# The low half of the w1 weights: a negated copy on ScalarE and a DMA that adds, in place of a subtraction on VectorE

## The chip, the cores and the metric

The kernel runs on one core of one Trainium2 chip. The metric is device time of one launch in microseconds (us); the median of three runs before the change is 1082.82 us (1081.4 to 1083.72). The core's engines are called PE (TensorE, the matrix unit; PEld is its weight load), DVE (VectorE), ACT (ScalarE), POOL (GpSimd) and SP (SyncE, which here does nothing but issue DMAs).

## What is computed

Two residual layers on an input of 512 tokens by 1024 features, all in float32. Layer 0 mixes tokens by a state-space scan and an attention with forget gates, layer 1 by a causal pooling and a gated unit. After each mixer stands a dense MLP with a squared ReLU, and that is where the change lies. Cut to what matters:

```python
for l in range(2):
    h = rms_norm(x, mix_pre_g[l])
    y = even_mixer(h, ...) if l % 2 == 0 else odd_mixer(h, ...)
    x = x + rms_norm(y, mix_post_g[l])
    h = rms_norm(x, mlp_pre_g[l])
    y = jnp.square(jax.nn.relu(h @ w1[l])) @ w2[l]     # w1: 1024 x 4096, w2: 4096 x 1024
    x = x + rms_norm(y, mlp_post_g[l])
```

## The kernel before, in words

**Two halves of every number.** PE multiplies in a float32 format of reduced precision (`fp32r`). To keep the precision, each operand is split in two: `hi`, the value rounded to fp32r, and `lo = value - hi`. `split` (line 611) does it: ACT copies the source to `hi`, which rounds, and DVE subtracts `hi` from the source into `lo`. `mm3` (line 620) then makes one product from three matmuls, hi by hi, hi by lo, lo by hi, accumulated in one PSUM bank.

**Weights.** A weight piece is a tile of 128 partitions by 1024 columns (512 KB). `class W` (line 634) takes three SBUF slots (`hi`, `lo`, `raw`), lets SP load the piece into `raw`, splits it, and frees `raw`. A w1 piece is the 1024 x 128 column block of w1 for 128 hidden features; in DRAM its rows are 128 floats, so it comes in 1024 runs of 512 bytes. There are 32 pieces for each of the two MLPs. w2 pieces are only loaded here (`Raw`); they are combined and split later.

**The MLP.** `mlp` (line 893) goes through four quarters of the hidden features. In each, eight times: take one w1 piece, compute its 128 x 512 hidden block (`block_T`, 24 matmuls), square the ReLU (`finish`), and between those blocks the second matrix product is done by seven block products in place of eight (`Seven`: `begin`, `corner`, and at the quarter's end `end` or, for the last quarter, `tail`). In the first quarter the first four pieces of MLP 0, three of MLP 1 (`FIRST`), are taken together, half of the tokens at a time, so that work can begin while the boundary before is still finishing.

**Order of the work.** Nothing runs when it is recorded. `Program.record` collects all operations, and `Program.issue` (line 284) simulates the five engines with fixed prices (`cost`, lines 242 to 282, and the latencies in `LAT`) and picks for each engine, one after the other, the ready operation of the best priority. The result is a fixed instruction order for every engine; on the chip each engine runs its list in that order and waits where an operand is not ready. A priority is made of the place in the program, the length of the chain that hangs on the operation, and hand-tuned boosts. In the planner's prices a 512 KB load on SP occupies the DMA for 1.6 us (`v.shape[0] * free(v) * 4 / 330`) and lands 2.0 us after that (lines 380 to 383, with 60 ns for the issue).

**Slots.** The tiles share 47 slots of 1024 columns and 4 of 512 (`Slots`, `Room`). A tile gets its slot when its first operation is picked, and how far a tile may run ahead of the oldest tile that has no slot yet is bounded by `LOOKS` (line 37): for loads, 7 tiles in MLP 0 (phase 1) and 13 in MLP 1 (phase 3). `take` and `getw` record up to `DEPTH` = 5 pieces ahead of their use.

**POOL's work.** In the MLPs POOL does almost nothing. At the layer boundaries it computes `1/sqrt` of the mean square (`rstd_of`, line 762), two small operations per norm.

Of the kernel before, what the change touches and what calls it, by code (L numbers as in the profile page):

```python
# [38 lines left out]
POOLF = 1  # L39
NWARM = 16  # L40
RANK = 0.55
DUE = 0.0
ORDER = "f z c q0 a0 u o q1 t s0 a1 s1 q2 a2 s2 q3 a3 s3".split()
ACTI = [3]
PBOOST = 4
# [121 lines left out]
class Program:  # L167
# [73 lines left out]
    @staticmethod  # L241
    def cost(eng, name, outs, ins, args, kw):
        def free(v):
            n = 1
            for x in v.shape[1:]:
                n *= x
            return n

        n = max([free(v) for v in outs[:1] + ins if v.shape[0] > 1 or len(ins) < 2] or [1])
        psum = any(v.t.bank for v in ins)  # L250
        if eng == "PE":
            out = outs[0]
            cols = free(out)
            if name == "transpose":
                return 109
            if ins[0].dtype == F32 and ins[0].t.dt != BF16:
                half = out.shape[0] <= 64 and ins[0].shape[0] <= 64
                return max(80, cols * 1.08) if half else cols * 1.7
            if ins[0].t.dt == BF16 or out.shape[0] <= 64:
                return max(53, cols / 2.4 + 3)  # L260
            return max(107, cols / 2.4 + 13.4)
        if eng == "ACT":
            ptr = sum(isinstance(kw.get(k), View) for k in ("bias", "scale", "accum_out"))
            return 0.833 * n + (51 if psum else 93) + 90 * ptr
        if eng == "DVE":
            if name == "reciprocal":
                return 6.3 * n + 60
            fast = name in ("tensor_copy", "tensor_scalar") and not psum
            ptr = 0
            if name in ("tensor_scalar", "scalar_tensor_tensor"):  # L270
                ptr = sum(isinstance(a, View) for a in args[2:4]) - (name == "scalar_tensor_tensor")
            return (0.52 if fast else 1.04) * n + 67 + 64 * ptr
        if eng == "POOL":
            if kw.get("op") == ALU.pow:
                return 464
            if name == "memset":
                return 0.83 * n + 36
            return 1.85 * n + 150 + 85 * (name == "tensor_scalar" and isinstance(args[2], View))
        if outs:
            v = outs[0]  # L280
            return v.shape[0] * free(v) * 4 / 330.0
        return 1600

    def issue(self):
# [7 lines left out]
                p.succs.append(o)  # L292
        for o in reversed(ops):
            o.rank = o.ns + max((s_.rank + self.LAT[o.eng][s_.eng] for s_ in o.succs), default=0.0)

        at = 0.0
        for o in ops:
            o.due = at
            if o.eng == "PE":
                at += o.ns  # L300
        for o in reversed(ops):
            own = o.due if o.eng == "PE" or not o.succs else math.inf
            o.due = min([own] + [s_.due - self.LAT[o.eng][s_.eng] - o.ns for s_ in o.succs])
        for o in ops:
            if o.eng != "SP":
                o.prio = (1 - DUE) * (o.prio * (1 - RANK) * UNIT - RANK * o.rank) + DUE * o.due - 1e3 * o.boost
                if o.banks and o.eng != "PE":
                    o.prio -= 1e3 * PBOOST
            for t in o.tiles:
                if t.pos is None:  # L310
                    t.pos = len(t.room.users)
                    t.room.users.append(t)
                    t.state, t.left = 0, len(t.ops)
                    t.used = {}
                    if t.bank:
                        t.needs = set(id(p) for u in t.ops if u.eng == "PE" for p in u.preds.values() if p.num < o.num)
# [32 lines left out]
        while len(order) < total:  # L349
            moved = True  # L350
            while moved:
                moved = False
                for e in self.engines:
                    if clock[e] > now:
                        continue
                    pick, best = None, None
                    for o in avail[e]:
                        if o.ready <= now and o.wake <= now and not (e == "SP" and head and o is not head[0]):
                            wake = 0.0
                            for t in o.banks:  # L360
                                for e2, end in t.used.items():
                                    if e2 != e:
                                        wake = max(wake, end + self.LAT[e2][e])
                            if wake > now:
                                o.wake = wake
                                heapq.heappush(events, (wake, len(order) + 0.75, None))
                                continue
                            key = o.prio
                            if e == "PE" and o.banks and o.banks[0].state == 1:
                                key -= STICKY * 1e3  # L370
                            if (best is None or key < best) and may(o):
                                pick, best = o, key
                    if pick is None:
                        continue
                    o = pick
                    avail[e].remove(o)
                    if o in head:
                        head.remove(o)
                    o.start = now
                    if e == "SP":  # L380
                        clock[e] = now + 60
                        dma = max(dma, now) + o.ns
                        o.end = dma + 2000
                    elif e == "PE":
                        while window < int(now / WINDOW):
                            slow, work = (2.0 if work < HAMT else 1.0), 0.0
                            window += 1
                        ns = o.ns
                        if half is not None and (half[1] <= o.half[0] or o.half[1] <= half[0]):
                            ns, half = min(ns, 67), None  # L390
                        else:
                            half = o.half
                        work += o.work
                        clock[e] = o.end = now + ns * slow
                    else:
                        clock[e] = o.end = now + o.ns
                    for t in o.tiles:
                        if t.state == 0:
                            t.room.take(t, e)
                        t.left -= 1  # L400
                        if not t.left:
                            t.room.give(t, self.LAT)
                    for t in o.banks:
                        t.used[e] = max(t.used.get(e, 0.0), o.end)
                    order.append(o)
                    moved = True
                    heapq.heappush(events, (o.end, len(order), o))
                    heapq.heappush(events, (clock[e], len(order) + 0.5, None))
                    for s_ in o.succs:
                        s_.ready = max(s_.ready, o.end + self.LAT[e][s_.eng])  # L410
                        s_.left -= 1
                        if not s_.left:
                            avail[s_.eng].append(s_)
                            heapq.heappush(events, (s_.ready, len(order) + 0.25, None))
            if len(order) == total:
                break
            if not events:
                raise RuntimeError("the schedule is stuck at " + str(len(order)))
            now = max(now, events[0][0])
            while events and events[0][0] <= now:  # L420
                o = heapq.heappop(events)[2]
                if o is not None:
                    done.add(id(o))
# [109 lines left out]
def tile_trunk(ctx: ExitStack, tc: tile.TileContext, x, mix_pre_g, mix_post_g, mlp_pre_g, mlp_post_g,  # L533
# [98 lines left out]


    class W:
        def __init__(self, src, shape):
            n = shape[0] * shape[1]
            self.shape = shape
# [4 lines left out]
            raw = arena.alloc(n)  # L642
            kept = boosted(f"W{prog.phase}")
            SP.dma_start(raw.f().rearrange("p (a b) -> p a b", a=shape[0]), src)
            split(raw.f(), self.b[0].r(), self.b[1].r())
            prog.boost = kept
            raw.free()

# [5 lines left out]
        def free(self):  # L654
            for b in self.b:
                b.free()

    class Raw:

# [26 lines left out]
    def plan_mlp(l):  # L686
        p = []
        for q in range(4):
            first = FIRST[l] if q == 0 else 0
            p += [rows(w1[l], 0, 8, 128 * j, 128) for j in range(first)]  # L690
            for j in range(8):
                if j >= first:
                    p.append(rows(w1[l], 0, 8, 128 * (8 * q + j), 128))
                for m_ in (int(c[1]) for c in AFTER[j].split() if c[0] == "b"):
                    p += [rows(w2[l], 128 * (8 * q + 2 * m_ + k), 1, 0, 1024) + (Raw,) for k in range(2)]
        return p
# [1259 lines left out]
```

## Time and profile before

| | |
|---|---|
| median of three runs | 1082.82 us (1081.4 to 1083.72) |
| the profiled execution | 1084.49 us |
| its span, first to last instruction | 1082.7 us |
| mean granted TensorE clock | 0.989 |
| instructions | 13916 |
| bytes read from HBM | 101.55 MB |

The page of the profile gives busy time by engine, the chain of work that ended last, groups of equal instructions with their mean duration, and DMA issues with the time to landing. Almost every instruction stands under line 429, the line of the planner that emits them, so the rows are told apart by engine, operation and shape: a row `b<-b,b 128x1024 fp32r<-128x1024 f32` on DVE is the subtraction of a split, `b<-b 128x1024 fp32r<-128x1024 f32` on ACT is its rounding copy. Since every engine's list is fixed, the n-th instruction of an engine in the trace is the n-th of its list, and so a single w1 piece can be followed through the trace from its load to the matmul that reads it. The two MLPs lie at about 277 to 577 us and 749 to 1071 us of the span.

### The profile page before, as it was taken

Reading aid. Unit: us, or ns where it says so; the run is one execution under the profiler, and the core shown is the slowest. Engines: PE = TensorE matmul, PEld = TensorE weight load, DVE = VectorE, ACT = ScalarE, POOL = GpSimd, SP = SyncE. Lnnn points to the kernel's source line nnn. Section 1 sums busy time; section 2 is a strip of 40 time slices with the busy share of each in tenths; the row PEclk is TensorE's granted clock in tenths of the full one; section 3 lists DMA queues with packets and bytes.
Section 4 is the critical chain, followed back from the end, with each engine's and each line's share of the span. In section 5 each row is a group of like instructions: output and inputs, shape, how many; then the busy total and the mean of one; then the engine's idle time right before and its main releaser. Section 6 shows DMA issues by size and latency. Waiting matters only on the chain.

```text
span 1082.7 us, 13916 instructions
## 1 busy us (share of the span) xinstructions
PE 1044.6 (96%) x5133; PEld 848.6 (78%) x5133; DVE 783.8 (72%) x1293; ACT 566.8 (52%) x1033; POOL 112.7 (10%) x238
## 2 busy tenths in 40 slices
PE   7979999999999999999999799999999999999997
PEld 4757877688988888888888578878888888888885
DVE  5955879858676497677677998757684686775786
ACT  5525877646474373454463654435663653553551
POOL 2892400003000000000000210011000000000001
PEclk9989999999999999999999899999999999999999
DMA  8122002353303233332423533307022424224302
GB/s 255 41 60 59 20 21 78 110 183 114 99 25 102 90 117 98 103 111 78 137 97 108 156 98 114 120 1 214 21 81 81 150 78 137 97 66 139 107 20 78
DMA packets 110386, 104.54 MB, mean 97 GB/s; under 512 B 9736, under 2 KB 92844, under 8 KB 110318
## 3 DMA queue, kind: packets, MB, share of 16 engines
q1 hardware_dynamic: 110318, 103.66, 31.0%
q8 instruction: 40, 0.66, 0.2%
q14 instruction: 28, 0.23, 0.1%
HBM read 101.55 MB, written 2.10 MB: 96 GB/s over the span
## 4 chain that ended last, share of the span: by engine, by line
PE 79%; DVE 8%; POOL 6%; ACT 3%; issue 2%; SPq 1%; DMA 1%; DVEq 0%; POOLq 0%; ACTq 0%
PE bank L429 79%; DVE b L429 7%; POOL b L429 4%; POOL small L429 2%; ACT junk L429 2%; ACT b L429 1%; SPq L429 1%; DMA b<-in_x_dram 1%; DVE small L429 0%; DVEq L1952 0%; POOLq L1952 0%; ACTq L429 0%; ACTq L1952 0%; DVEq L429 0%; POOLq L429 0%
## 5 line engine op out<-in xcount | busy, mean ns | idle before, releaser
L429 PE MATMUL bank<-b,b 128*128 128x512 f32 (+5 forms) x4684 | 1003.6, 377 | 16.1 <-DVE b L429 6.7
L429 PEld LDWEIGHTS bank<-b,b 128*128 128x128 f32 (+2 forms) x4684 | 812.0, 188 | 190.4 <-ACT b L429 10.2
L429 DVE TENSOR_TENSOR b<-b,b 128x512 fp32r<-128x512 f32 (+5 forms) x622 | 475.7, 800 | 131.1 <-ACT b L429 61.5
L429 ACT ACTIVATE b<-b 128x1024 fp32r<-128x1024 f32 (+6 forms) x578 | 376.0, 693 | 289.1 <-PE bank L429 144.0
L429 ACT ACTIVATE b<-bank 128x512 f32<-128x512 f32 (+6 forms) x269 | 130.3, 515 | 133.5 <-PE bank L429 126.2
L429 DVE TENSOR_TENSOR b<-bank,b 128x512 f32<-128x512 f32 (+4 forms) x210 | 121.0, 602 | 58.5 <-PE bank L429 39.3
L429 DVE TENSOR_TENSOR b<-b 128x512 f32<-128x512 f32 (+3 forms) x164 | 81.4, 503 | 43.0 <-PE bank L429 20.7
L429 POOL TENSOR_SCALAR small<-small 128x1 f32<-128x1 f32 x36 | 17.3, 480 | 589.7 <-ACT junk L429 568.6
L429 PE MATMUL bank<-ct,b 128*128 128x128 f32 (+3 forms) x387 | 43.9, 264 | 13.5 <-DVE b L429 12.9
L429 PEld LDWEIGHTS bank<-ct,b 128*128 128x128 f32 (+3 forms) x387 | 34.2, 141 | 26.9 <-issue 11.9
L429 DVE SCALAR_TENSOR_TENSOR b<-b,small,b 128x1024 f32<-128x1024 f32 (+1 forms) x32 | 36.4, 1149 | 20.8 <-POOL small L429 20.7
L429 ACT ACTIVATE junk<-b 128x512 bf16<-128x512 f32 (+1 forms) x32 | 27.0, 845 | 45.1 <-DVE b L429 36.9
L429 POOL MEMSET b<- 128x4 f32 (+5 forms) x29 | 9.3, 355 | 345.2 <-PE bank L429 292.4
L429 POOL TENSOR_TENSOR b<-b,b 128x8 f32<-128x8 f32 (+6 forms) x84 | 42.0, 521 | 0.3
L429 ACT ACTIVATE b<-bank,small 128x256 f32<-128x256 f32 (+4 forms) x36 | 19.2, 543 | 16.2 <-DVE small L429 13.0
L429 DVE SCALAR_TENSOR_TENSOR b<-b,b 128x512 f32<-128x512 f32 (+2 forms) x28 | 19.0, 685 | 11.7 <-ACT b L429 11.1
L429 POOL TENSOR_TENSOR small<-small,mhalf 128x1 f32<-128x1 f32 x36 | 22.6, 629 | 3.0
L429 DVE TENSOR_REDUCE small<-bank 128x1 f32<-128x128 f32 (+3 forms) x32 | 13.9, 483 | 9.3 <-PE bank L429 9.1
L429 ACT ACTIVATE junk<-bank 128x512 bf16<-128x512 f32 x16 | 9.5, 596 | 18.9 <-PE bank L429 14.0
L429 POOL TENSOR_TENSOR b<-b 128x16 f32<-128x16 f32 x40 | 15.1, 379 | 5.4 <-DVE b L429 5.0
L429 DVE TENSOR_SCALAR b<-b,small 128x128 f32<-128x128 f32 (+3 forms) x28 | 12.0, 443 | 3.1 <-POOL small L429 2.5
L429 DVE SCALAR_TENSOR_TENSOR b<-b,bank 128x512 f32<-128x512 f32 x16 | 10.9, 681 | 2.7 <-ACT b L429 2.6
(43 smaller groups left out, 117.4 us busy)
## 6 DMA issues: line engine op xcount, KB each, us to landing
b<-in_mlp_w_dram SPq DMA_DIRECT2D x128, 512.0 KB, 4.3
b<-in_w_in_even_dram SPq DMA_DIRECT2D x16, 512.0 KB, 6.7
b<-in_w_in_odd_dram SPq DMA_DIRECT2D x12, 512.0 KB, 4.0
b<-in_w_out_even_dram SPq DMA_DIRECT2D x8, 512.0 KB, 3.5
b<-in_w_out_odd_dram SPq DMA_DIRECT2D x8, 512.0 KB, 3.5
b<-in_x_dram SPq DMA_DIRECT2D x7, 512.0 KB, 6.0
out_dram<-b SPq DMA_DIRECT2D x8, 256.0 KB, 2.0
b<-in_s_w_glu_dram SPq DMA_DIRECT2D x2, 512.0 KB, 3.6
```

The source lines that it names most:

```text
L429: o.ins = o.fn(*args, **kw)
```

## The change

w1 pieces that are not among the first four (MLP 0) or three (MLP 1), 28 and 29 of 32, are made by a new class `Added`. SP still loads `raw`, ACT still writes `hi`. The subtraction on DVE is gone: ACT writes `lo = -raw`, rounded like `hi`, so that `lo = -hi`, and a DMA issued from POOL's queue reads the piece from DRAM a second time and adds it to `lo`, which gives `raw - hi`. The planner prices that DMA on POOL at 1000 ns, 1600 ns of DMA time, and a landing 2500 ns after that. The parameter `DUE`, which was 0.0, and the lines that computed due times are removed; with 0.0 they had no share in a priority.

```diff
@@ cost
         if eng == "POOL":
+            if name == "dma_start":
+                return 1000
@@ issue
-        at = 0.0
-        for o in ops:
-            o.due = at
...
-                o.prio = (1 - DUE) * (o.prio * (1 - RANK) * UNIT - RANK * o.rank) + DUE * o.due - 1e3 * o.boost
+                o.prio = o.prio * (1 - RANK) * UNIT - RANK * o.rank - 1e3 * o.boost
@@ issue
                         o.end = dma + 2000
+                    elif o.name == "dma_start":
+                        clock[e] = now + o.ns
+                        dma = max(dma, clock[e]) + 1600
+                        o.end = dma + 2500
@@ class W
+        by_dma = False
+
...
-            split(raw.f(), self.b[0].r(), self.b[1].r())
+            hi, lo = (b.r() for b in self.b)
+            if self.by_dma:
+                act(hi, raw.f(), AF.Copy)
+                act(lo, raw.f(), AF.Copy, scale=-1.0)
+                G.dma_start(lo.rearrange("p (a b) -> p a b", a=shape[0]), src, accum_op=ALU.add)
+            else:
+                split(raw.f(), hi, lo)
...
+    class Added(W):
+
+        by_dma = True
@@ plan_mlp
                 if j >= first:
-                    p.append(rows(w1[l], 0, 8, 128 * (8 * q + j), 128))
+                    p.append(rows(w1[l], 0, 8, 128 * (8 * q + j), 128) + (Added,))
```

More of the change, by code (lines that the diff above doesn't have):

```diff
@@ L41 @@
 RANK = 0.55
-DUE = 0.0
 ORDER = "f z c q0 a0 u o q1 t s0 a1 s1 q2 a2 s2 q3 a3 s3".split()
@@ L294, in issue @@
             o.rank = o.ns + max((s_.rank + self.LAT[o.eng][s_.eng] for s_ in o.succs), default=0.0)
-        at = 0.0
-        for o in ops:
-            o.due = at
[L299 to L303, printed above, removed]
         for o in ops:
             if o.eng != "SP":
-                o.prio = (1 - DUE) * (o.prio * (1 - RANK) * UNIT - RANK * o.rank) + DUE * o.due - 1e3 * o.boost
+                o.prio = o.prio * (1 - RANK) * UNIT - RANK * o.rank - 1e3 * o.boost
                 if o.banks and o.eng != "PE":
```

## Prediction

> **What bounds the kernel now.** I read the page's busy line first, then a table of stretches, then the chain of waits, then what PE waited for inside an MLP.
>
> ```profile
> PE 1044.6 (96%) x5133; PEld 848.6 (78%) x5133; DVE 783.8 (72%) x1293; ACT 566.8 (52%) x1033; POOL 112.7 (10%) x238
> ```
>
> PE is busy nearly always. The average says nothing of the place, so the table: us of the stretch, then busy us and instructions of PE, PEld, DVE, ACT and POOL, the granted clock, the DMA share and GB/s. The rows are MLP 0, MLP 1, the boundary behind MLP 0 and the one ahead of MLP 1.
>
> ```profile
> 277.00:577.00 300.00, 299.77 (x1374) 247.89 (x1375) 210.95 (x312) 156.71 (x258) 0.33 (x3) 1.00 0.30 93
> 749.00:1071.00 322.00, 321.59 (x1444) 264.41 (x1445) 228.72 (x339) 163.64 (x273) 1.93 (x4) 1.00 0.28 89
> 577.00:627.00 50.00, 42.18 (x180) 33.02 (x178) 41.64 (x55) 24.60 (x42) 9.28 (x16) 0.93 0.49 146
> 696.00:749.00 53.00, 51.29 (x264) 42.81 (x262) 31.69 (x43) 22.17 (x47) 8.03 (x16) 1.00 0.26 79
> ```
>
> In both MLPs PE has no idle time to speak of (299.77 of 300, 321.59 of 322) at full clock. DVE is busy for 70% of MLP 0 and still holds nobody up. The chain that ended last says the same: two unbroken stretches of PE.
>
> ```profile
> 277.23 307.94 PE bank L429 x1408
> ...
> 749.41 321.62 PE bank L429 x1443
> ```
>
> The table of waits, cut to 300 to 575 us, has one row for PE: who waited for whom, us in total, times, longest.
>
> ```profile
> PEld bank L429 <- DVE b L429: 1.0, 5, 0.3
> ```
>
> All that MLP 0's PE loses to DVE is 1.0 us. The change takes work from DVE in just those stretches where DVE is not the limit.
>
> **What goes, what comes.** In the groups of the same stretch (count, busy us, mean ns, idle before) the subtraction of a 1024-column split and its rounding copy are these:
>
> ```profile
> L429 DVE TENSOR_TENSOR b<-b,b 128x1024 fp32r<-128x1024 f32 x67 | 81.1, 1221 | 30.2 <-PE bank L429 24.4 <-ACT b L429 4.9
> L429 ACT ACTIVATE b<-b 128x1024 fp32r<-128x1024 f32 x65 | 67.8, 1057 | 58.6 <-PE bank L429 31.0 <-DVE b L429 24.4 <-DMA b<-in_mlp_w_dram 3.1
> ```
>
> DVE loses 57 subtractions of 1.221 us, 69.6 us in all, off the path but for that 1.0 us. ACT gets 57 copies of 1.057 us, 60.2 us; in MLP 0 that takes it from 156.7 to 186.3 us of 300, and it stays hidden under PE. Operations queued behind a second copy on ACT, the ReLU and squares of a finished block among them, move by 1.06 us; ACT's own waits above are mostly for PE, so I cost that at nothing.
>
> The load on SP stays as it is, and `raw` comes free at the second copy, about when it did. The second transfer's queue is POOL's: its instruction waits there for ACT, and behind it could stand only the norm's small operations at a boundary. MLP 0's stretch has 0.33 us of POOL work, so nobody is behind it there. At MLP 1's start the first pieces fall among POOL operations of the chain; one transfer ahead of one of them costs 0 to about 1 us. The planner sees that conflict, and I take 0.
>
> One more operation per piece also shifts the numbers by which the planner ranks all later work, so its lists will differ in places that have nothing to do with w1; I take 0 for that and keep 2 us to either side. `DUE` was zero, and its removal changes no priority.
>
> DMA room is no limit. In MLP 0 the loads' queue (packets, MB, share of 16 engines) and the loads (count, size, us to landing) stand so:
>
> ```profile
> q1 hardware_dynamic: 30032, 27.79, 29.9%
> ...
> b<-in_mlp_w_dram SPq DMA_DIRECT2D x53, 512.0 KB, 4.1
> ```
>
> 29.9% of 16 engines over 300 us is 1435 engine-us for 27.79 MB, so 512 KB (0.524 MB) take 27.1 engine-us, 1.7 us on all 16. Reading 28 pieces again adds 14.7 MB, and reading what stands in the tile as much once more: the share would go to about 61%.
>
> **Where it can cost: the low half is ready later.** Today it is ready 1.22 us of DVE after `hi`, plus waiting. With the change there follow on `hi`: a second copy of 1.06, the hand-over to POOL and on to PE (the planner's 0.06 and 0.22), POOL's issue, the transfer. By the planner's prices issue, transfer and landing are 1.0 + 1.6 + 2.5 = 5.1, so 6.44 us in all, and it arranges PE's list for that. What exceeds 5.1 on the chip it does not know, and PE, which keeps its order, waits for it where a piece has no reserve.
>
> No POOL DMA is in this trace. From below: POOL's 1.0 and a landing like a load's 4.1 make 5.1, the planner's own figure, an excess of 0. A POOL part below 1.0 would make it less than nothing, which adds reserve and no time. From above: an addition must read the tile as well as DRAM, 1.7 us more by the rate above. I take that value, because both reads pass the same 16 engines: the excess is 1.7 us. [...]
>
> How much reserve has a piece? I followed every w1 piece of MLP 0 from the end of its `hi` copy on ACT to PE's first weight load from `lo`, and the shortest are these (start, duration): the 22nd piece, with its load and its subtraction, then the 6th and the 15th.
>
> ```profile
> 456.27 0.38 SPq L429 DMA_DIRECT2D b<-in_mlp_w_dram  x1
> 460.85 1.04 ACT L429 ACTIVATE b<-b 128x1024 fp32r<-128x1024 f32 x1
> 462.99 1.22 DVE L429 TENSOR_TENSOR b<-b,b 128x1024 fp32r<-128x1024 f32 x1
> 465.72 0.19 PEld L429 LDWEIGHTS bank<-b,b 128*128 128x128 f32 x1
> ...
> 293.48 1.05 ACT L429 ACTIVATE b<-b 128x1024 fp32r<-128x1024 f32 x1
> 299.49 0.19 PEld L429 LDWEIGHTS bank<-b,b 128*128 128x128 f32 x1
> ...
> 383.70 1.05 ACT L429 ACTIVATE b<-b 128x1024 fp32r<-128x1024 f32 x1
> 390.03 0.19 PEld L429 LDWEIGHTS bank<-b,b 128*128 128x128 f32 x1
> ```
>
> That is 465.72 - 461.89 = 3.8 us, 5.0 and 5.3, all under 6.44. The same subtraction for all 28, the 5th to the 32nd, of which these are the first and the last,
>
> ```profile
> 264.35 1.04 ACT L429 ACTIVATE b<-b 128x1024 fp32r<-128x1024 f32 x1
> 294.04 0.19 PEld L429 LDWEIGHTS bank<-b,b 128*128 128x128 f32 x1
> ...
> 549.21 1.06 ACT L429 ACTIVATE b<-b 128x1024 fp32r<-128x1024 f32 x1 [1.05 <-DVE b L429]
> 564.38 0.19 PEld L429 LDWEIGHTS bank<-b,b 128*128 128x128 f32 x1
> ```
>
> gives, in the order of use: 28.6, 5.0, 8.6, 6.9, 8.4, 12.4, 17.8, 10.4, 15.6, 9.4, 5.3, 7.6, 9.6, 16.4, 23.9, 7.85, 13.7, 3.8, 9.0, 8.1, 7.5, 18.5, 26.0, 11.7, 17.7, 9.1, 13.7, 14.1. The three below 6.44 the planner must bring into order; it has the quarter's closing products to put ahead of such a block, so I cost that at nothing, but their reserve is then zero. The rest keep what is over 6.44. An excess of 1.7 us then shows at four places: at the 6th piece 1.7 (which gives it to the three behind), at the 15th 1.7, at the 20th (7.85, reserve 1.4) 0.3, at the 22nd 1.7. Sum: 5.4 us.
>
> In MLP 1, where loads may run 13 tiles ahead, the shortest is
>
> ```profile
> 845.92 1.06 ACT L429 ACTIVATE b<-b 128x1024 fp32r<-128x1024 f32 x1 [3.72 <-PE bank L429]
> 856.91 0.19 PEld L429 LDWEIGHTS bank<-b,b 128*128 128x128 f32 x1
> ```
>
> 9.9 us, a reserve of 3.5, more than the excess: nothing is lost there.
>
> The profiled execution took 1084.49 us (span 1082.7), 1.67 above the median. 1084.49 + 5.4 = 1089.9 for such an execution, and 1082.82 + 5.4 = 1088.2 us for the median. A small gain elsewhere cannot pay for it: the 1.0 us of waits for DVE is the whole store in MLP 0.
>
> **Rival 1: hidden.** The addition lands like a load, the excess is 0, the planner's order holds. For it: a load needs 4.1 us in this stretch, 1.7 of it moving bytes, so even some more would vanish in reserves like 8 or 9 us. Against it: three pieces have none. 1083 us, within 2.
>
> **Rival 2: faster.** PE idles 7.8 us behind MLP 0 (42.18 of 50), where DVE is busiest (41.64 of 50). If `raw` slots come free a little sooner and DVE's list holds less, the list after MLP 0 may close up; a third of that idle time would be 2.6 us, 1080.2 us. Against it: the last subtraction that goes ends well before 577 us, and what fills DVE in that stretch are splits of layer 1's weights and the norms, which stay. It decides if the first loads of layer 1's weights, now after 582 us by the row below, come before 577.
>
> ```profile
> L429 SPq DMA_DIRECT2D b<-in_w_in_odd_dram x12: 367/373/1565, 582.3 to 642.0; - x12
> ```
>
> [...]
>
> **How the numbers follow.** A repeated measurement of this kernel can tell about 0.2%, 2.2 us. Forecast 0.40, rival 1 0.25, rival 2 0.15, rival 3 0.20. The forecast's own range is 1085 to 1094 us (an excess of about 0.8 to 3 us). The whole range, 1080 to 1108 us, takes in rival 1, most of rival 2 and rival 3 up to its worked price; outside lie a POOL that is slower still and an order that closes up better. Faster by over 0.2%: rival 2 and 0.02 of rival 1, 0.17. Within: 0.23 of rival 1 and 0.02 of the forecast, 0.25. Slower: the rest, 0.58.
>
> **What would show it.** In the profile after: DVE's busy time down by about 70 us and ACT's up by about 60, if the change does what it says; a POOL DMA row whose issue and landing together exceed 5.1 us; in MLP 0 new rows of PEld waiting for a DMA, 5 us in all, at three or four places; none in MLP 1. If landing is near 5 us and PE has no such waits, rival 1 holds. [...] The forecast is wrong if PE waits in MLP 1 too, or if the time moves without any new wait.

## The result and the profile after

The change made the kernel slower: a median of 1106.59 us in four runs (1105.28 to 1108.26) beside 1083.27 us for the kernel before (1081.4 to 1084.85). The ratio is 1.0214 [1.0202, 1.0227], some 23.2 us, where 5.4 had been forecast. The profiled execution took 1108.26 us with a span of 1106.5, 23.8 us more than the one of before; its mean granted clock fell from 0.989 to 0.982.

The busy line and the two DMA queues (packets, MB, share of 16 engines) of the page after come first. The planner's helper line is now line 425.

```profile
PE 1052.2 (95%) x5133; PEld 851.3 (77%) x5133; DVE 722.9 (65%) x1236; ACT 615.6 (56%) x1090; POOL 202.2 (18%) x295
...
q1 hardware_dynamic: 110318, 103.66, 30.3%
q0 software_dynamic: 59280, 29.89, 22.0%
```

The edit did what it says: 57 operations left DVE (1293 to 1236, 60.9 us less; about 70 were forecast) and 57 came to ACT (48.8 us more; about 60 were forecast, and the second copy of a pair starts 0.95 us after the first, so the two overlap a little). PE has as many matmuls as before, is busy 7.6 us longer and idle for the rest. The table of stretches, in the columns of before, shows where; the rows are MLP 0, MLP 1 (which now begins some 18 us later) and the 50 us in which the boundary behind MLP 0 lay before (it now begins some 14 us later, so the third row is the same time and not the same work).

```profile
277.00:577.00 300.00, 290.53 (x1311) 237.61 (x1312) 163.53 (x257) 168.96 (x268) 42.31 (x30) 0.99 0.69 140
767.00:1089.00 322.00, 317.50 (x1415) 260.07 (x1415) 195.64 (x307) 184.86 (x296) 43.10 (x29) 0.99 0.66 136
577.00:627.00 50.00, 40.99 (x181) 32.70 (x179) 43.01 (x61) 27.04 (x47) 7.94 (x12) 0.92 0.40 123
```

In the 300 us of MLP 0 PE did 1311 matmuls in place of 1374; 63 matmuls at 300/1374 us each are 13.8 us. It idled 9.5 us there, against 0.2 before. In MLP 1 it idled 4.5 us, against 0.4. By stages, from the first w1 matmul of one to the next stage's, MLP 0 with its boundary grew from 359.8 to 377.6 us, MLP 1 from 334.4 to 340.2, and layer 1 between them stayed (112.6, 112.4). Who made PE wait stands in the table of waits from 277 us to the end:

```profile
PEld bank L425 <- DMA b<-in_mlp_w_dram: 14.5, 9, 3.7
...
PE bank L425 <- DMA b<-in_mlp_w_dram: 10.7, 7, 3.3
```

These are the new waits that the prediction named, but twice as long (10.7 us, seven times), and one of them, of 2.3 us at 1030 us, is in MLP 1. The largest is the 22nd piece's. The timeline shows POOL's issue for it, then PE:

```profile
464.43 1.55 POOL L425 DMA_DIRECT2D b<-in_mlp_w_dram  x1 [13.03 <-ACT b L425]
```

```profile
469.71 2.15 PE L425 MATMUL bank<-b,b 128*128 128x512 f32 x8 [0.81 <-ACT b L425]
475.12 7.16 PE L425 MATMUL bank<-b,b 128*128 128x512 f32 x23 [3.26 <-DMA b<-in_mlp_w_dram]
```

POOL was free and began at 464.43, the transfer landed at 475.07, 10.65 us later, and PE went on at 475.12. The planner had allowed 5.1 us. The groups of the page and the DMA issues (count, size, median us from issue to landing) show that this is no exception:

```profile
L425 POOL DMA_DIRECT2D b<-in_mlp_w_dram x57 | 89.0, 1562 | 494.8 <-ACT b L425 387.0
...
b<-in_mlp_w_dram SPq DMA_DIRECT2D x128, 512.0 KB, 5.2
b<-in_mlp_w_dram POOLq DMA_DIRECT2D x57, 512.0 KB, 8.1
```

A transfer lands 8.1 us after its issue begins, 3.0 over the plan, and plain loads land later too (5.2 us; 4.3 on the page of before). In MLP 0 the landings run from 6.41 to 12.46 us, in MLP 1 from 6.45 to 16.39; 21 of the 57 take over 9 us. The longest come in bursts, when ACT releases several at once after a stretch in which PE held it up. Ahead of these four ACT had waited 11.13 us for PE, and they landed after 11.35, 15.5, 16.4 and 15.9 us:

```profile
1018.97 1.55 POOL L425 DMA_DIRECT2D b<-in_mlp_w_dram  x1 [25.00 <-ACT b L425]
1020.87 1.55 POOL L425 DMA_DIRECT2D b<-in_mlp_w_dram  x1 [0.35 <-ACT b L425]
1022.76 1.55 POOL L425 DMA_DIRECT2D b<-in_mlp_w_dram  x1 [0.34 <-ACT b L425]
1026.42 1.57 POOL L425 DMA_DIRECT2D b<-in_mlp_w_dram  x1 [2.10 <-DMA b<-in_mlp_w_dram]
```

What one transfer costs follows from the queue's row: 22.0% of 16 engines over 1106.5 us are 3895 engine-us, by 59280 packets 65.7 ns each, and by 57 transfers and 16 engines 4.27 us. (The records of several transfers overlap in time: the DMA share in the rows below reaches 1.44. So 4.27 is record time, not time in which nothing else moves.) With the issue of 1.56 that leaves 2.3 of the 8.1 us for landing and queueing. The trace's packet records show the queueing: in the burst of four the first packet of each transfer starts when the last one of the transfer before it has ended (first packets at 1021.54, 1027.52, 1033.53 and 1038.24 us, last ends at 1027.58, 1033.58, 1038.29 and 1041.74).

The stalls cost more than their length. The stretches behind the 22nd piece (475.5 us), the 25th (516.5) and the one in MLP 1 (1031.9) show the granted clock at half; the row behind the 6th piece's stall of 1.43 us does not.

```profile
475.50:478.90 3.40, 3.40 (x10) 2.62 (x9) 0.86 (x2) 1.43 (x2) 0.92 (x1) 0.50 1.18 229
516.50:519.80 3.30, 3.30 (x9) 2.65 (x8) 0.00 (x0) 0.99 (x1) 0.00 (x0) 0.50 1.44 180
1031.90:1035.10 3.20, 3.20 (x9) 2.53 (x8) 1.78 (x3) 1.29 (x2) 0.00 (x0) 0.50 1.29 228
302.50:305.90 3.40, 3.40 (x15) 2.81 (x16) 3.40 (x6) 3.25 (x4) 0.00 (x0) 1.00 0.74 92
```

After gaps of 3.26, 2.06 and 2.32 us PE ran some 3.4 us at half clock, so each lost about 1.7 us more. Ahead of these three stretches (from 475.46, 516.42 and 1031.83 us, 3.41 us long) PE had been idle for 3.08, 2.06 and 1.95 us of the last 3.41, still at full clock. In the clock records of this trace and of the one of before, the changes lie multiples of 3.41 us apart. Of the steps of that length at full clock, from 230 us to the end of MLP 1 (1068 us before; 1090 after), six had PE idle for 1.95 to 3.23 us, and each was followed by one at half clock; the rest had 1.41 us or less, and none was. The length of a gap alone doesn't decide: the gap of 4.32 us at 607.04 us of before lay across two steps; behind the first, with 1.41 us of idle time in all, the clock stayed full, behind the second, with 3.22 us, it was half.

### The profile page after: what moved, and what is told of

It reads as the page before. It is cut to its first block, busy times and chain, and to the rows that moved or that the text cites. A ratio compares the mean times of both kernels' runs of the same rounds, so it can differ in the third digit from the quotient of the medians.

```text
span 1106.5 us, 14086 instructions
## 1 busy us (share of the span) xinstructions
PE 1052.2 (95%) x5133; PEld 851.3 (77%) x5133; DVE 722.9 (65%) x1236; ACT 615.6 (56%) x1090; POOL 202.2 (18%) x295
## 3 DMA queue, kind: packets, MB, share of 16 engines
q0 software_dynamic: 59280, 29.89, 22.0%
## 5 line engine op out<-in xcount | busy, mean ns | idle before, releaser
L425 PE MATMUL bank<-b,b 128*128 128x512 f32 (+5 forms) x4684 | 1008.5, 378 | 25.8 <-DMA b<-in_mlp_w_dram 10.7
L425 ACT ACTIVATE b<-b 128x1024 fp32r<-128x1024 f32 (+6 forms) x635 | 425.7, 723 | 261.8 <-PE bank L425 133.6
L425 DVE TENSOR_TENSOR b<-b,b 128x1024 fp32r<-128x1024 f32 (+6 forms) x565 | 409.5, 759 | 164.8 <-ACT b L425 106.5
L425 POOL DMA_DIRECT2D b<-in_mlp_w_dram x57 | 89.0, 1562 | 494.8 <-ACT b L425 387.0
L425 DVE TENSOR_TENSOR b<-b 128x256 f32<-128x256 f32 (+3 forms) x164 | 81.8, 506 | 65.0 <-ACT b L425 25.3
L425 PE MATMUL bank<-ct,b 128*128 128x128 f32 (+3 forms) x387 | 46.4, 274 | 19.6 <-DVE b L425 16.8
L425 ACT ACTIVATE junk<-bank 128x512 bf16<-128x512 f32 x16 | 9.5, 595 | 18.0 <-PE bank L425 13.7
L425 DVE SCALAR_TENSOR_TENSOR b<-b,bank 128x512 f32<-128x512 f32 x16 | 10.9, 683 | 5.8 <-ACT b L425 5.7
```

The costliest lines, as they stand in the source:

```text
L425: o.ins = o.fn(*args, **kw)
```

## The experiments

My first theory (in the expectations A) was that the second half simply lands later than the planner believed, so that the cure lies in its prices. Its rivals: the second read's traffic delays everything, whatever the plan (D); the seven tiles that loads may run ahead in MLP 0 are too few (E); the boundary's order is what is lost (F); the second ACT copy or the changed order, without any transfer, make the time (B); and it is POOL's longer issue that is late (C). All ratios are to the kernel before, run on the same chip.

**No transfer at all.** The instruction lists are those of the changed kernel, but the DMA isn't emitted.

```diff
-            o.ins = o.fn(*args, **kw)
+            if o.name != "dma_start" or o.eng == "SP":
+                o.ins = o.fn(*args, **kw)
```

> The changed kernel's lists, with the adding DMA left out where the planner would emit it: lo stays minus hi, so the result is not the reference's. No second transfer, no landing to wait for, ACT's second copy and the order stay. Theory F (order of the lists costs about 4 us, the transfer the rest): 1086 to 1089 us, as with the plain copy. If the plain copy's 4 us were its landings: 1082 to 1085.

It took 1085.26 us, ratio 1.0014 [1.0005, 1.0023], +1.5 us. MLP 0 is whole again:

```profile
277.00:577.00 300.00, 299.12 (x1379) 247.88 (x1379) 177.68 (x278) 180.13 (x285) 0.94 (x5) 1.00 0.30 93
```

So the ACT copies, the new order and the relief of DVE come to 1.5 us together, so theory B falls, and the rest belongs to the transfer. Behind MLP 0 PE's gaps add to 10.1 us without a transfer, as good as the 10.6 with it and above the 8.2 of before, so what the boundary lost in idle time lies in the lists.

**The same transfer without the addition.** POOL's DMA overwrites `lo` in place of adding; the lists stay.

```diff
-                G.dma_start(lo.rearrange("p (a b) -> p a b", a=shape[0]), src, accum_op=ALU.add)
+                G.dma_start(lo.rearrange("p (a b) -> p a b", a=shape[0]), src)
```

> The changed kernel, every engine's list the same, but POOL's DMA copies the piece over lo and adds nothing (so lo holds the weight itself and the result is not the reference's). Theory A (the adding transfer lands later than the planner's 5.1 us, 8.1 median, and PE waits for it): a copy should move its 512 KB in about 1.7 us in place of 4.3, land about 5.6 us after the issue starts, and PE's waits for it in MLP 0 fall from 8.4 us to under 2; 1084 to 1090 us. Theory B (the lists themselves are worse): PE waits move little, 1100 to 1107 us. Theory C (POOL's issue of 1.56 us is what is late): about 1100 us.

1089.15 us, 1.0041 [1.0027, 1.0055], +4.4 us. Its page:

```profile
q0 software_dynamic: 59280, 29.89, 16.5%
...
L425 POOL DMA_DIRECT2D b<-in_mlp_w_dram x57 | 50.4, 884 | 509.4 <-ACT b L425 379.1
...
b<-in_mlp_w_dram POOLq DMA_DIRECT2D x57, 512.0 KB, 5.7
```

The issue is 0.88 us in place of 1.56, a packet 48.5 ns in place of 65.7 (16.5% of 16 × 1089.4 us by 59280), a transfer 3.15 us on 16 engines in place of 4.27, and the landing 5.7 us, 0.6 over the plan. PE waits 2.2 us for landings in place of 10.7:

```profile
PE bank L425 <- DMA b<-in_mlp_w_dram: 2.2, 3, 1.2
```

**The addition over long runs.** The adding DMA reads 128 runs of 4 KB from w2; the lists stay.

```diff
-                G.dma_start(lo.rearrange("p (a b) -> p a b", a=shape[0]), src, accum_op=ALU.add)
+                G.dma_start(lo, w2[0][0:128, 0:1024], accum_op=ALU.add)
```

> The changed kernel, lists the same, but the adding DMA reads 128 rows of 4 KB (of w2) in place of 1024 runs of 512 bytes, so what it adds is not the weight and the result is not the reference's. [...] If adding costs by the byte: landing stays near 8 and the time near 1106.

1095.74 us, 1.0118 [1.0096, 1.0141], +12.8 us, below the time near 1106 that was expected if adding costs by the byte; the landing fell from 8.1 to 7.1 us.

```profile
q0 software_dynamic: 8208, 29.89, 15.6%
...
L425 POOL DMA_DIRECT2D b<-in_mlp_w_dram x57 | 49.7, 871 | 517.1 <-ACT b L425 391.1
...
b<-in_mlp_w_dram POOLq DMA_DIRECT2D x57, 512.0 KB, 7.1
```

With the same lists in all four, the median landing and the loss go together: no transfer +1.5, 5.7 us +4.4, 7.1 us +12.8, 8.1 us +23.2. PE's waits for landings go the same way: none, 2.2, 4.7 and 10.7 us. Of the 23.2 us the addition itself is 18.8, a plain transfer from POOL's queue 2.9, the order and the copies 1.5. An addition over long runs was as cheap to issue as a plain copy (0.87 and 0.88 us) and took a like time of the engines (2.99 and 3.15 us), yet it landed 1.4 us later. By the packet records most of that lies between the first packet and the end of the last, 3.8 us in the median against 2.7 of the plain copy; the time from the issue to the first packet is alike (2.1 and 2.0). So a shorter issue alone does not cure it, and theory C falls.

**DVE adds what is already there.** The order of operations per piece is the change's, but the second read is replaced by an addition on DVE.

```diff
-                G.dma_start(lo.rearrange("p (a b) -> p a b", a=shape[0]), src, accum_op=ALU.add)
+                add(lo, raw.f(), lo.bitcast(F32))
```

> The changed kernel without the DMA: ACT still writes minus the weight, and DVE adds raw to it (one DVE operation of 1.22 us again, one ACT copy of 1.06 more than before). It prices ACT's second copy and the longer ACT part of the chain alone. Theories A and D: 1082 to 1086 us, the ACT copy is hidden. If ACT were what costs: 1090 or more.

1085.23 us, 1.0007 [0.9998, 1.0017]: the second ACT copy costs nothing that can be told.

**The measured prices.** The planner gets what the profile after shows.

```diff
-                return 1000
+                return 1560
...
-                        dma = max(dma, clock[e]) + 1600
-                        o.end = dma + 2500
+                        dma = max(dma, clock[e]) + 4270
+                        o.end = dma + 2300
```

> The changed kernel with the planner's price of the transfer set to what the trace shows: 1.56 us on POOL, 4.27 us of DMA, landing 2.3 us later, 8.1 in all. Theory A (late landings that the planner does not know of): the lists are rearranged so that the direct waits go, 1083 to 1090 us. Theory D (the doubled traffic on the 16 DMA engines delays the other loads, whatever the order): 1095 us or more, with waits for split w2 weights in their place. Theory B (chance of the order): anywhere, without the direct waits going.

1100.98 us, 1.0146 [1.0125, 1.0167]. By stages, MLP 0 and MLP 1:

```profile
277.00:577.00 300.00, 288.94 (x1306) 236.33 (x1306) 166.57 (x261) 169.29 (x264) 42.16 (x30) 0.99 0.69 140
767.00:1089.00 322.00, 321.15 (x1445) 264.18 (x1443) 199.79 (x312) 186.99 (x300) 43.77 (x31) 1.00 0.66 137
```

MLP 1's loss is gone, MLP 0's is not. Right prices suffice in MLP 1, where loads may run 13 tiles ahead; theory A as I had put it, for both, fell, and the time lies where D had put it (1095 or more).

**Only MLP 1**, first with the change's prices, then with the measured ones.

```diff
-                    p.append(rows(w1[l], 0, 8, 128 * (8 * q + j), 128) + (Added,))
+                    p.append(rows(w1[l], 0, 8, 128 * (8 * q + j), 128) + ((Added,) if l else ()))
```

> Only MLP 1's w1 pieces are made by the adding DMA; MLP 0 is as before. By the account of the two traces MLP 1 lost 5.8 us and MLP 0 with the boundary behind it 17.8: theory A says 1085 to 1090 us, as most pieces of MLP 1 have 15 us and more in reserve; theory D (traffic) says half of the loss, about 1094.

> The adding DMA in MLP 1 alone, priced as measured. Mispriced it cost 6.6 us. Theory A (only what the planner does not know is waited for): 1083 to 1086 us, no difference from the kernel before. Theory D: still 5 us or more.

With the change's prices it took 1091.24 us, 1.0061 [1.0046, 1.0077], a little above the 1085 to 1090 that A had given: MLP 1's +6.6 us stands by itself. With the measured ones it took 1083.33 us, 0.9997 [0.9986, 1.0007]:

```profile
747.00:1069.00 322.00, 321.09 (x1439) 263.99 (x1439) 199.13 (x312) 186.84 (x300) 43.72 (x31) 1.00 0.66 136
```

The landings are as late as ever (7.8 us in the median) and the DMA share is 0.66, but PE waits for none of them. So the traffic alone costs nothing where the plan knows of it, which speaks against D in this stage. And 29.6 us less work on DVE (228.72 to 199.13 of 322) gained nothing.

**Further ahead in MLP 0.** The measured prices, and loads may run 9, then 13 tiles ahead in MLP 0.

```diff
-LOOKS = {1: (51, 21, 7), 2: (100, 8, 13), 3: (38, 20, 13)}
+LOOKS = {1: (51, 21, 9), 2: (100, 8, 13), 3: (38, 20, 13)}
```

> The changed kernel, the transfer priced as measured (8.1 us in all), and MLP 0's loads allowed to run 9 tiles ahead in place of 7. Theory E (in MLP 0 the prices alone did not help because a load cannot start early enough there; MLP 1, with 13 tiles, lost nothing once priced): some of the 16 us that the priced kernel still lost comes back, 1086 to 1095 us. Theory D (traffic on the DMA engines in bursts): about 1100 as with 7.

> The same with 13 tiles ahead, MLP 1's figure. Theory E: MLP 0 loses no more than MLP 1 did with true prices, 1084 to 1090 us. Theory D: about 1100. If 13 is no better than 9, reserve is not what is missing.

With 9 it took 1087.29 us, 1.0037 [1.0023, 1.0052], and one wait for a landing was left, the first fence below. With 13 it took 1097.7 us, 1.0128 [1.0109, 1.0147], with two, the second; E had said 1084 to 1090.

```profile
PE bank L425 <- DMA b<-in_mlp_w_dram: 2.0, 1, 2.0
```

```profile
PE bank L425 <- DMA b<-in_mlp_w_dram: 6.5, 2, 3.9
```

Theory E holds only half: room ahead can remove most of the loss, yet more room is not better. D, which had said about 1100 for both, fails with 9, where the same transfers are made, but not with 13. That the planner writes another order with every setting, and that it is chance of this order whether a late landing meets a matmul that needs it, is my reading; no run separates it from a part of the traffic in MLP 0.

**The kernel before with 9 tiles ahead**, the subtraction on DVE as it was.

```diff
-LOOKS = {1: (51, 21, 7), 2: (100, 8, 13), 3: (38, 20, 13)}
+LOOKS = {1: (51, 21, 9), 2: (100, 8, 13), 3: (38, 20, 13)}
```

> The kernel before with 9 tiles ahead in MLP 0: the control for that number. 1082 to 1087 us; only if it is itself 4 us off does it explain the priced kernel with 9 tiles.

1085.13 us, 1.0013 [1.0004, 1.0021]. So some 1.4 us of the 9-tile version's loss come with the setting itself, and the transfer's part of it is 1.0037 less 1.0013, about 2.6 us.

**The last quarter of MLP 0 left on DVE**, with the measured prices and 9 tiles, to see whether the list ahead of the boundary holds the remainder.

```diff
-                    p.append(rows(w1[l], 0, 8, 128 * (8 * q + j), 128) + (Added,))
+                    p.append(rows(w1[l], 0, 8, 128 * (8 * q + j), 128) + ((Added,) if l or q < 3 else ()))
```

> As the priced kernel with 9 tiles ahead, but the last quarter of MLP 0 keeps the subtraction on DVE, so that the planner's list at the boundary behind MLP 0 should be like the one before. Theory F (what that kernel still loses, 4 us, is the boundary's list: PE idles 9.5 us there in place of 8.2, and at half clock for longer): 1082 to 1085 us. Theory E (still missing reserve in MLP 0): 1086 to 1088 as with all four quarters.

1086.27 us, 1.0032 [1.0021, 1.0043]: no different from all four quarters. A wait of 1.31 us for a landing was left at 452.7 us, ahead of that quarter, and theory F, which had said 1082 to 1085, fell.

**Where DVE is busiest.** w1 goes back to DVE as before, and four of layer 1's input pieces, at the boundary, are made by the adding DMA, with the measured prices.

```diff
-                    p.append(rows(w1[l], 0, 8, 128 * (8 * q + j), 128) + (Added,))
+                    p.append(rows(w1[l], 0, 8, 128 * (8 * q + j), 128) + ())
...
-    plan += [rows(wo, 0, 8, 128 * j, 128) for j in range(4)]
+    plan += [rows(wo, 0, 8, 128 * j, 128) + (Added,) for j in range(4)]
```

> The adding DMA not for w1 at all but for four pieces of layer 1's input weights, split where DVE is busiest (41.6 of 50 us) and PE idles 7.8 us; priced as measured. If DVE's relief pays anywhere it is here: up to 2.6 us less, 1080 to 1082 us. If the boundary is a chain of norms that DVE's other work doesn't lengthen: 1082 to 1086. If POOL's 1.56 us issues get ahead of the norms' POOL operations: 1086 or more.

1082.03 us, 0.9986 [0.9977, 0.9996], 1.5 us less than the kernel before, on the border of two expected outcomes. The stretch at the boundary, first of before, then of this kernel:

```profile
592.00:632.00 40.00, 31.71 (x139) 24.93 (x138) 35.08 (x50) 22.92 (x42) 9.16 (x16) 0.91 0.46 128
```

```profile
592.00:632.00 40.00, 31.70 (x142) 24.92 (x141) 30.85 (x46) 26.41 (x46) 13.42 (x20) 0.91 0.87 177
```

DVE has 4.2 us less to do there, but PE is busy just as long. So these rows don't show that DVE's relief makes the gain; the gain is below what one comparison of this kernel can tell with any safety.

## Why the prediction was wrong

**Right in kind.** PE is the limit, relief for DVE in the MLPs is worth nothing (0.9997 with MLP 1 moved and planned for), the second copy on ACT is hidden (1.0007), and the loss is PE waiting for late low halves. Three of the four places named have it: the 6th piece waits 1.43 us, the 20th 0.59, the 22nd 3.26. The 15th has none, its neighbour the 16th waits 0.68, and the 8th (0.41) and 25th (2.06) come on top.

**The step that failed first: "the excess is 1.7 us".** One figure stood for every piece. It measured 3.0 in the median, 1.3 at the least and 11 at the most. I took POOL's issue at the planner's 1.0 us and it is 1.56. I took the second read of the tile as equal to the first, so 3.4 us on 16 engines, and it is 4.27. I took one transfer to find the engines free, and the bursts queue: the mean share, forecast at 61%, was 0.69 in MLP 0, but 1.10 from 450 to 475 us, around the longest stall. In POOL's own queue a packet of the adding transfer took 65.7 ns, one of the plain copy 48.5, a ratio of 1.35. What I had missed is that the plain copy there, 3.15 us, is already well above the 1.7 us of a load from SP's queue. By the packet records of that run a 512-byte packet took 49 ns there and 30 in SP's queue. Whether the queue makes that difference stays open: POOL's transfer also goes from float32 into a tile that the kernel declares as fp32r (`lo`), SP's does not (`raw`), and no run separates the two.

As a single figure for every piece, though, the excess explains at most half of the loss. With 3.0 in place of 1.7 the prediction's own sum gives 3.0 at the 6th, 15th and 22nd piece, 1.6 at the 20th and 0.3 at the 30th, 10.9 us in all and 1093.7 us, still inside its range. The waits in MLP 0 came to 8.4 us. The rest of the 23.2 us is what the sum held at nothing:

**"Nothing is lost there" for MLP 1 failed.** It lost 5.8 us. The reserve of 3.5 us was measured on single pieces of the old order, while a burst is 6 to 11 us over the plan. PE waited 2.32 us for one piece, a step at half clock followed, and two splits held PE for 1.6 us (1.00 at 911 us, 0.60 at 986); ahead of both ACT had waited for a load (2.15 us and 0.96).

**Two terms were not in the sum.** The three stalls of 2.06, 2.32 and 3.26 us in the MLPs cost about 1.7 us more each by the half clock behind them. And behind MLP 0 the boundary lost some 4 us: its gaps went from 8.2 to 10.6 us, and the half clock after them grew from two stretches of 3.4 us to one of 13.7. Without a transfer the same lists have gaps of 10.1 us and 10.2 us at half clock, and MLP 0 with its boundary takes 2.7 us longer than before (MLP 1 is 1.5 us shorter in that run), so the larger part of the 4 us comes with the lists.

**"I take 0" for the shifted lists** measured 1.5 us, inside the 2 us that I had kept to either side. The sum by stages: 13.8 in MLP 0, some 4 at its boundary, 5.8 in MLP 1, -0.2 in layer 1, 23.4 of the 23.8 us between the two profiled executions.

**The rivals.** The third one had POOL as the slow part. The result lies near the upper end of the range, which reached up to that one's price, but no run shows a POOL issue long enough to make it: with DVE busy for 65% of the span, the longest of the 57 took 1.75 us, 0.75 over the planner's price. The tile's row gives least, median and most in ns:

```profile
L425 POOL DMA_DIRECT2D b<-in_mlp_w_dram x57: 1540/1550/1753, 265.7 to 1043.5; - x57
```

The excess came from the transfer and its queue. Rival 1 would have needed a landing near 5 us; even the plain copy took 5.7. Rival 2's mechanism is not here, since DVE's work at the boundary didn't get shorter (41.64 us of the 50 before; 42.37 from 591 to 641 us, where this stretch now lies).

## What to carry to other kernels

Work moved from an engine that holds nobody up to a DMA gained nothing here, and where the result was ready later than planned, the fixed instruction order turned that into waits of the engine that binds, 10.7 us of PE's. Before a new kind of transfer goes into a plan, measure its issue, its time on the engines and its landing, alone and in a burst: the same addition with right prices cost nothing in one MLP (0.9997), and with wrong ones 6.6 us. Count a stall of PE with the clock that it loses: here stalls of 2.06, 2.32 and 3.26 us each cost about 1.7 us more, and one of 1.43 us nothing more.

## What was not expected of the hardware

- From POOL's queue a plain copy of 512 KB in 512-byte runs, float32 into fp32r, took 3.15 us on 16 engines by its packet records; loads from SP's queue, w1 and w2 together and float32 throughout, took 1.7.
- POOL's issue: 0.88 us for a plain copy in 1024 runs, 0.87 us for an addition in 128 runs, 1.56 us for an addition in 1024 runs.
- An addition landed 8.1 us after its issue began in the median, 6.4 at best and 16.4 in a burst of four, whose packets went one transfer after the other (first packets at 1021.54, 1027.52, 1033.53 and 1038.24 us).
- In the traces of before and after, PE's clock was halved behind each of six 3.41 us steps in which PE had idled 1.95 us or more, and behind none with 1.41 us or less.
